# First keys of a hybrid layer's memory projection: one transfer or two, and their place in two queues

## The chip, the cores and the metric

The kernel runs on one core of a Trainium2 chip. The metric is the device time of one execution in microseconds. TensorE (PE in the profile, its weight loads PEld) multiplies; VectorE is DVE, ScalarE ACT, GpSimd POOL; SyncE (SP) issues most of the DMA transfers. A line such as L445 is a line of the kernel before.

## The reference, cut to what matters

```python
h = rms_norm(x, norm_g)                      # x: 256 tokens of 1024 channels
(qa, ka, va, ga, ub, vb, gb, qc, gc, ma, mb, mc) = split_cols(h @ w_in, IN_SPLITS)
out_a = moba_attention(rope(qa), rope(ka), va) * silu(ga)          # 6 heads
out_b = gmlp_spatial_gate(ub, vb, ln_g, w_spatial, b_spatial) * silu(gb)
mk, mv = split(rms_norm(mem, mem_norm_g) @ w_mem_kv, 2, axis=-1)   # 256 memory tokens, 2 x 512 columns
out_c = softmax(qc @ mk.T * 128 ** -0.5) @ mv * silu(gc)           # 4 heads
y = sigmoid(ma) * (out_a @ w_a) + sigmoid(mb) * (out_b @ w_b) + sigmoid(mc) * (out_c @ w_c)
out = rms_norm(x + y @ w_out, final_norm_g)
```

All is float32. The change concerns the loads for the product of the memory tokens with `w_mem_kv`, whose left half of columns gives the memory's keys (mk) and whose right half its values (mv), and one piece of `w_in`.

## The kernel before, in words

Every float32 product is made from three passes: each operand is split into a high part that TensorE takes at its fast float32 format (ACT copies it, "hi") and the remainder (DVE subtracts, "lo"), and high x high, high x low and low x high are summed in PSUM. So each slice of weights goes through the same string: it lands by DMA, ACT makes its high part, DVE its low part, TensorE uses both.

The work is a list of 128 chunks, worked off in order by TensorE. Chunks 0 to 7 ("mvk") are the memory's keys and values: the 1024 channels are cut into 8 slices of 128, and HALVES gives the order of value and key slices: chunk 0 is the first values and the first keys, chunk 1 the second values and keys, and so on. Chunks 8 to 11 ("tok") and all later ones multiply the layer's own tokens with pieces of `w_in` ("fea" chunks, 128 output columns each, and "st" chunks, which form products of two-by-two blocks from seven factors), then come the three branch products and the output product.

A slice of the array `mw` holds, for 128 channels, 256 memory tokens, 512 value columns and 512 key columns (slice 0 has 16 columns of gains ahead of them). Tokens and values go to the tile `st` (two tiles, of four slices each, by `load_st`, L311), the keys to the first raw pieces, `raw[2]` and `raw[3]` (by `load_wk`, L325 and, for the last two slices together, L323). Slice 0's tokens and values come in two transfers, the tokens with the first 256 value columns on SP's queue and the other 256 on ACT's. Slice 1's tokens and values (384 KB) come on ACT's queue, everything else on SP's, in the order in which the loop at the end of this section's listing issues it: keys of slice 0, keys of slice 1, then for each further slice the tokens and values and then the keys, with two rows of x in between.

In the first chunks `split_mvk` makes the engines' work: the memory tokens are multiplied with their gains and split (DVE in chunks 0 to 2: L435 the high part, L430 the low part; later ACT makes the high part at L427), and `half_hi` (ACT, L445) and `half_lo` (DVE, L449) split the values and the keys. For chunk 0 `half_hi` works on two halves of 256 columns. TensorE multiplies values at L525 (into the banks "aux") and keys at L531 (into "acc"). While the first load is under way TensorE runs eight matmuls on constants (L377).

The other pieces of `w_in` ("raw", 128 rows of 2048 columns, two chunks each, 1 MB) are loaded by `load` at L220 into three buffers as these come free; pieces 12 to 21 come as two halves of 512 KB, the others whole. Piece 12 holds the "fea" chunks q4 and k4, and `split_hi` at L274 makes their high parts. The order of all this work behind the first chunks is set when the program is built by a planner (`Units`) with its own estimates of durations; it knows nothing of the transfers of the first slices but a few fixed times.

Each DMA issued by SP or ACT is given one of eight landing semaphores (DMAHW0 to DMAHW7) in turn. An issue that gets a semaphore for a second time waits until the transfer that had it before has landed.

Of the kernel before, what the change touches and what calls it, by code (L numbers as in the profile page):

```python
# [42 lines left out]
NG = 2 * KD  # L43
# [110 lines left out]
def tile_hybrid_layer(ctx: ExitStack, tc: tile.TileContext, mw, xT, mem, x, fin_g, ln_g, w, ws, w_sp, b_sp, b_spt, rope, out):  # L154
    nc = tc.nc
# [9 lines left out]
    def slot_tile(name, shape, tag, dt=F32):  # L165
        V[name] = act.tile(shape, dt, name=name, tag=tag)
        return V[name]
# [22 lines left out]
    raw, hi, lo = {}, {}, {}  # L190
# [24 lines left out]
    def raw_alloc(j):  # L215
        raw[j] = wts.tile([128, PIECE], F32, name="raw", tag="raw", bufs=RAW)

    def load_part(j, a, b):
        src = bass.AP(tensor=w.tensor, offset=w.offset + (j - 4) * 128 * PITCH + a, ap=[[PITCH, 128], [1, b - a]])
        nc.sync.dma_start(raw[j][:, a:b], src)  # L220

    def load(j):
        raw_alloc(j)
        parts = 2 if 12 <= j < 22 else 1
        for i in range(parts):
            load_part(j, i * PIECE // parts, (i + 1) * PIECE // parts)

# [25 lines left out]
    def buf(g, i):  # L253
        return FORMS[i][0] ^ (g % 2)
# [36 lines left out]
    XW = S + 512  # L291
# [8 lines left out]
    def slice_k(k, a, b):  # L300

        row = NG + XW + 512
        return bass.AP(tensor=mw.tensor, offset=mw.offset + 128 * row * k + a, ap=[[row, 128], [1, b - a]])

    def load_st(queue, k, a, b):

        o = 0 if k < 4 else -NG - 4 * XW
        a, b = (a and a + NG, b + NG) if k == 0 else (a, b)
        src = slice_k(k, a, b)
        o += NG + k * XW if k else 0  # L310
        queue.dma_start(st[k // 4][:, o + a:o + b], src)  # L311
# [5 lines left out]
    def load_wk(queue, k):  # L317
        o = XW if k else NG + XW
        if k == KD - 1:
            row = NG + XW + 512  # L320
            src = bass.AP(tensor=mw.tensor, offset=mw.offset + 128 * row * (k - 1) + o,
                          ap=[[row, 128], [128 * row, 2], [1, 512]])
            queue.dma_start(raw[3][:, 1024:2048].rearrange("p (k n) -> p k n", k=2), src)  # L323
        elif k < KD - 2:
            queue.dma_start(raw[2 + k // 4][:, (k % 4) * 512:(k % 4) * 512 + 512], slice_k(k, o, o + 512))  # L325

    def load_x(parts=1):
        slot_tile("xk", [128, 2, D], "xr")
        for i in range(parts):
            rows = slice(2 * i // parts, 2 * (i + 1) // parts)  # L330
            nc.sync.dma_start(V["xk"][:, rows, :], x[:, 0:2 * D].rearrange("p (t d) -> p t d", t=2)[:, rows, :])

    def load_x_row(t):
        if t == 0:
            slot_tile("xk", [128, 2, D], "mr")
        nc.sync.dma_start(V["xk"][:, t, :], x[:, t * D:t * D + D])
# [8 lines left out]
    load_st(nc.sync, 0, 0, S + 256)  # L345
    load_st(nc.scalar, 0, S + 256, XW)
    nc.scalar.preload_act_table(AF.Sqrt)
    load_st(nc.scalar, 1, 0, XW)
    for k in range(KD):
        if k > 1:  # L350
            load_st(nc.sync, k, 0, XW)
        load_wk(nc.sync, k)
        if k in (4, 5):
            load_x_row(k - 4)
    load_xt(0)
# [890 lines left out]
    for c in range(n_br):  # L1246
        if chunks[c][0] == "st":
            _, g, i, h = chunks[c]
            b = buf(g, i)
# [5 lines left out]
    for c in range(n_br + 4):  # L1255
# [4 lines left out]
        if c == n_br - 8:  # L1260
            load_x()
# [21 lines left out]
        for d in (0, LATER) if s in place else ():  # L1283
            q, odd = divmod(2 * place[s][0] + place[s][1] - 1 - d, 2)
            q += 2
            if not odd and 4 < q < len(PLAIN) // 2 and (q in LATE) == (d > 0):
                load(q)
                if q == 6:
                    load_mem()
# [132 lines left out]
```

## Time and profile before

| | |
|---|---|
| median of 3 runs | 312.42 us (312.19 to 313.19) |
| the profiled execution's own time | 311.98 us |
| its span | 310.3 us |
| PE busy | 304.0 us, 98% |
| PEld busy | 258.5 us, 83% |
| DVE busy | 269.5 us, 87% |
| ACT busy | 232.6 us, 75% |
| mean granted TensorE clock | 0.996 |

The span runs from the first to the last instruction; the execution's own time has some microseconds around it. In a timeline's row stand the start, the busy time, the engine, the line, the operation and out<-in; brackets give the engine's idle time ahead of it and what ended that. An engine's name with a q (SPq, ACTq) is its sequencer, which issues DMAs. The chain of work that ended last is followed back from the last instruction, at each step to what released it.

### The profile page before, as it was taken

What the parts mean: (1) busy time and instruction counts of PE and PEld (TensorE: products, weight loads), DVE (VectorE), ACT (ScalarE), POOL (GpSimd) and SP (SyncE); (2) the same over time, 40 slices, a digit from 0 to 9 for tenths busy, and PEclk for the clock granted to TensorE, in tenths of its full rate; (3) what the DMA queues carried; (4) which work ended last, traced back from release to release, by engine and by line L of the source; (5) the groups of instructions that cost most, each with busy time, mean ns of one, the idle gap of its engine ahead of it and who ended that gap; (6) DMA issues with size and microseconds to landing.
All of it is one profiled execution on the core that took longest, in us unless ns stands there. A gap on an engine that the chain in (4) does not pass through costs nothing.

```text
span 310.3 us, 4528 instructions
## 1 busy us (share of the span) xinstructions
PE 304.0 (98%) x1570; PEld 258.5 (83%) x1570; DVE 269.5 (87%) x391; ACT 232.6 (75%) x373; POOL 35.8 (12%) x55
## 2 busy tenths in 40 slices
PE   8999999999999999999999999999999999999993
PEld 4888888889888888888888888888888888888982
DVE  3989999899879999898699899999896898989532
ACT  5877999766797865888999996698659666586333
POOL 1000040040011013005013002004011031000022
PEclk9999999999999999999999999999999999999998
DMA  7999999659959869959949959969996999953003
GB/s 283 396 407 413 419 281 299 247 82 183 371 191 274 251 212 208 286 201 208 343 125 196 259 230 278 212 219 209 210 374 126 296 328 219 372 207 136 2 0 135
DMA packets 20598, 75.14 MB, mean 242 GB/s; under 512 B 2656, under 2 KB 3936, under 8 KB 18144
## 3 DMA queue, kind: packets, MB, share of 16 engines
q1 hardware_dynamic: 15824, 58.35, 51.5%
q0 software_dynamic: 4320, 15.73, 28.2%
q10 hardware_dynamic: 432, 0.79, 0.7%
q8 instruction: 12, 0.20, 0.2%
q14 instruction: 10, 0.08, 0.1%
HBM read 73.02 MB, written 1.05 MB: 239 GB/s over the span
## 4 chain that ended last, share of the span: by engine, by line
PE 97%; DMA 1%; ACT 1%; issue 0%; DVE 0%; ACTq 0%
PE acc L658 27%; PE acc L593 19%; PE aux L593 12%; PE acc L471 6%; PE acc L473 6%; PE acc L472 6%; PE acc L531 4%; PE aux L525 4%; PE aux L472 2%; PE aux L473 2%; PE aux L471 2%; PE aux L825 2%; PE acc L504 2%; PE aux L504 2%; DMA st<-in_mw_dram 1%; PE aux L1058 1%
## 5 line engine op out<-in xcount | busy, mean ns | idle before, releaser
L274 ACT ACTIVATE hi<-form 128x1024 fp32r<-128x1024 f32 x70 | 73.0, 1059 | 32.4 <-DMA form<-in_ws_dram 17.9
L277 DVE TENSOR_TENSOR lo<-form,hi 128x1024 fp32r<-128x1024 f32 x70 | 84.4, 1219 | 11.7 <-ACT hi L274 11.6
L277 DVE TENSOR_TENSOR lo<-raw,hi 128x1024 fp32r<-128x1024 f32 x58 | 70.1, 1221 | 6.5 <-ACT hi L274 6.2
L274 ACT ACTIVATE hi<-raw 128x1024 fp32r<-128x1024 f32 x58 | 61.1, 1059 | 9.9 <-PE acc L473 4.8
L658 PE MATMUL acc<-n,hi 128*128 128x512 f32 x240 | 59.8, 392 | 0.0
L244 POOL DMA_DIRECT2D form<-in_ws_dram x30 | 26.1, 875 | 225.1 <-DVE lo L277 78.6
L658 PEld LDWEIGHTS acc<-n,hi 128*128 128x128 f32 x240 | 44.1, 188 | 8.6
L658 PEld LDWEIGHTS acc<-n,lo 128*128 128x128 f32 x240 | 31.4, 191 | 1.4
L658 PE MATMUL acc<-n,lo 128*128 128x256 f32 x240 | 32.5, 283 | 0.0
L593 PE MATMUL acc<-hi,s 128*128 128x512 f32 x96 | 32.3, 394 | 0.0
L593 PE MATMUL acc<-hi,n 128*128 128x512 f32 x72 | 24.2, 395 | 0.0
L593 PEld LDWEIGHTS acc<-hi,s 128*128 128x128 f32 x96 | 18.0, 188 | 3.5
L593 PE MATMUL aux<-hi,s 128*128 128x512 f32 x64 | 20.7, 389 | 0.0
L593 PE MATMUL acc<-lo,s 128*128 128x512 f32 x48 | 18.7, 390 | 0.0
L593 PE MATMUL aux<-hi,n 128*128 128x512 f32 x48 | 15.9, 391 | 0.0
L593 PEld LDWEIGHTS acc<-hi,n 128*128 128x128 f32 x72 | 13.5, 188 | 2.7
L593 PEld LDWEIGHTS aux<-hi,s 128*128 128x128 f32 x64 | 12.0, 188 | 2.6
L593 PE MATMUL acc<-lo,n 128*128 128x512 f32 x36 | 14.1, 390 | 0.0
L593 PE MATMUL aux<-lo,s 128*128 128x512 f32 x32 | 12.5, 389 | 0.0
L248 DVE TENSOR_TENSOR form<-form,form 128x1024 f32<-128x1024 f32 x10 | 12.2, 1219 | 0.0
L593 PEld LDWEIGHTS aux<-hi,n 128*128 128x128 f32 x48 | 9.0, 188 | 1.8
L593 PEld LDWEIGHTS acc<-lo,s 128*128 128x128 f32 x48 | 9.0, 188 | 1.5
(262 smaller groups left out, 607.5 us busy)
## 6 DMA issues: line engine op xcount, KB each, us to landing
raw<-in_w_dram SPq DMA_DIRECT2D x18, 1024.0 KB, 8.2
form<-in_ws_dram SPq DMA_DIRECT2D x30, 512.0 KB, 5.4
form<-in_ws_dram POOLq DMA_DIRECT2D x30, 512.0 KB, 8.6
raw<-in_w_dram SPq DMA_DIRECT2D x22, 512.0 KB, 6.9
st<-in_mw_dram SPq DMA_DIRECT2D x6, 384.0 KB, 6.7
raw<-in_mw_dram SPq DMA_DIRECT2D x6, 256.0 KB, 5.6
xk<-in_x_dram SPq DMA_DIRECT2D x2, 512.0 KB, 6.9
xt<-in_xT_dram SPq DMA_DIRECT2D x2, 512.0 KB, 8.9
```

Of the source, the lines that this page charges most:

```text
L244: nc.gpsimd.dma_start(form_half(i, h), block(g, b, h), accum_op=OP.add)
L248: nc.vector.tensor_tensor(form_half(i, h), form_half(i, h), form_half(1 - i, h), OP.add)
L274: nc.scalar.activation(hi[c][:, a:b], source(c)[:, a:b], AF.Copy)
L277: nc.vector.tensor_tensor(lo[c][:, a:b], source(c)[:, a:b], hi[c][:, a:b].bitcast(F32), OP.subtract)
L471: nc.tensor.matmul(p, s_hi, m_hi, start=first, stop=False)
L472: nc.tensor.matmul(p, s_hi, m_lo, start=False, stop=False)
L473: nc.tensor.matmul(p, s_lo, m_hi, start=False, stop=last)
L504: nc.tensor.matmul(acc[name, o][t], src[:, k0 + i, tsl(t)], wt[c][:, i * 512:(i + 1) * 512], start=c == 8 and i + j == 0, stop=c == 11 and ...
L525: nc.tensor.matmul(acc["mv", 0][t][:, a:b], src[:, k, tsl(t)], wt[:, a:b], start=k + n == 0, stop=k == KD - 1 and n == len(parts) - 1)
L531: nc.tensor.matmul(p, wt, m, start=k == 0 and j < HC, stop=k == KD - 1 and j >= HC)
L593: nc.tensor.matmul(p, x[:, k0 + k, tsl(t)], wt[c][:, a * 512:(a + 1) * 512], start=first and a + j == 0, stop=half == 1 and a + j == 3, sk ...
L658: nc.tensor.matmul(o, wt, m, start=i == 0, stop=i == len(passes) - 1, skip_group_check=True)
```

## The change

The first slice's keys, one transfer of 256 KB on SP's queue before, become two of 128 KB: columns 0 to 255 on SP's queue, columns 256 to 511 on ACT's. On ACT's queue that half stands ahead of the second slice's tokens and values. And piece 12 of `w_in` is loaded whole, as one transfer of 1 MB, where it came in two.

```diff
     def load(j):
         raw_alloc(j)
-        parts = 2 if 12 <= j < 22 else 1
+        parts = 2 if 13 <= j < 22 else 1
...
+    def load_wk_first(queue, a, b):
+        queue.dma_start(raw[2][:, a:b], slice_k(0, NG + XW + a, NG + XW + b))
+
...
     load_st(nc.sync, 0, 0, S + 256)
     load_st(nc.scalar, 0, S + 256, XW)
     nc.scalar.preload_act_table(AF.Sqrt)
+    load_wk_first(nc.sync, 0, 256)
+    load_wk_first(nc.scalar, 256, 512)
     load_st(nc.scalar, 1, 0, XW)
     for k in range(KD):
         if k > 1:
             load_st(nc.sync, k, 0, XW)
-        load_wk(nc.sync, k)
+        if k:
+            load_wk(nc.sync, k)
```

How the instructions stand: on SP, the program's first loads before, with the semaphores that each issue waits for in brackets (`st` are tokens and values, `raw` the keys, 528 columns are slice 0's gains, tokens and first values):

```order
L311 DMA st_72<-in_mw_dram 128x528
L325 DMA raw<-in_mw_dram 128x512 x2
L311 DMA st_72<-in_mw_dram 128x768
L325 DMA raw<-in_mw_dram 128x512
L311 DMA st_72<-in_mw_dram 128x768
L325 DMA raw<-in_mw_dram 128x512 [waits DMAHW0_49]
L311 DMA st_73<-in_mw_dram 128x768 [waits DMAHW1_49]
```

And the same place on SP now:

```order
L311 DMA st_72<-in_mw_dram 128x528
L328 DMA raw<-in_mw_dram 128x256
L325 DMA raw<-in_mw_dram 128x512
L311 DMA st_72<-in_mw_dram 128x768
L325 DMA raw<-in_mw_dram 128x512
L311 DMA st_72<-in_mw_dram 128x768 [waits DMAHW0_49]
L325 DMA raw<-in_mw_dram 128x512 [waits DMAHW1_49]
```

The first key transfer has half its columns. With one transfer more in the turn of the eight semaphores, the first issue that waits is the fourth slice's tokens and values (it waits for slice 0's second transfer), where it was the fourth slice's keys. On ACT, the program's start before (its queue and its work; the two DMAs are slice 0's other values and slice 1):

```order
L311 DMA st_72<-in_mw_dram 128x256
L347 ACT_TABLE_LOAD
L311 DMA st_72<-in_mw_dram 128x768
L445 ACTIVATE hi<-st_72 128x256 [waits DMAHW1_49]
L445 ACTIVATE hi<-st_72 128x256 [waits DMAHW0_49]
L445 ACTIVATE hi<-raw 128x256 [waits DMAHW2_49]
L445 ACTIVATE hi<-raw 128x256
L445 ACTIVATE hi<-st_72 128x512 [waits DMAHW4_49]
```

And the same place on ACT now:

```order
L311 DMA st_72<-in_mw_dram 128x256
L350 ACT_TABLE_LOAD
L328 DMA raw<-in_mw_dram 128x256
L311 DMA st_72<-in_mw_dram 128x768
L451 ACTIVATE hi<-st_72 128x256 [waits DMAHW1_49]
L451 ACTIVATE hi<-st_72 128x256 [waits DMAHW0_49]
L451 ACTIVATE hi<-raw 128x256 [waits DMAHW2_49]
L451 ACTIVATE hi<-raw 128x256 [waits DMAHW4_49]
L451 ACTIVATE hi<-st_72 128x512 [waits DMAHW6_49]
```

ACT issues one DMA more, ahead of slice 1; its work stands in the same order, and the second half of the first keys now waits for a landing of its own. On SP around piece 12 (`form` are sums of weight blocks, `mid` the rotary embedding's moves):

```order
 L220 DMA raw<-in_w_dram 128x2048 x2
-L241 DMA form_403<-in_ws_dram 128x1024
+L241 DMA form_404<-in_ws_dram 128x1024
+L220 DMA raw<-in_w_dram 128x2048
+L241 DMA form_404<-in_ws_dram 128x1024
+L819 DMA mid<-qk 32x256 x4
 L220 DMA raw<-in_w_dram 128x1024 x2
-L241 DMA form_403<-in_ws_dram 128x1024
-L813 DMA mid<-qk 32x256 x4
```

Piece 12 is one issue of 2048 columns at the same place; what follows stands as before (the next pair of halves is piece 13).

## The prediction

> **What bounds the kernel now.** I read the page's busy times first, then the list of waits of TensorE's weight loads, then the chain of work that ended last over the first 12 us, and only then the single engines in that stretch.
>
> ```profile
> span 310.3 us, 4528 instructions
> PE 304.0 (98%) x1570; PEld 258.5 (83%) x1570; DVE 269.5 (87%) x391; ACT 232.6 (75%) x373; POOL 35.8 (12%) x55
> ```
>
> TensorE is busy for 98% of the span, so a change to loads can only win where TensorE waits for them. The waits of its weight loads from 0 to 300 us say where that is (columns: total us, times, longest):
>
> ```profile
> PEld L377 <- issue: 2.5, 7, 0.8
> PEld aux L525 <- ACT hi L445: 0.7, 1, 0.7
> PEld acc L531 <- DVE lo L449: 0.3, 1, 0.3
> PEld acc L531 <- ACT hi L445: 0.3, 1, 0.3
> PEld aux L525 <- DVE lo L449: 0.2, 1, 0.2
> ```
>
> L377 is the warming up. The other four are all there are, and the chain (start, length, what) puts them at the start:
>
> ```profile
> 0.81 2.95 DMA st<-in_mw_dram
> 3.78 0.43 ACT hi L445
> 4.28 1.76 PE aux L525 x8
> 6.04 1.62 PE acc L531 x8
> 7.66 1.40 PE aux L525 x6
> 9.06 1.39 PE acc L531 x8
> 10.45 1.37 PE aux L525 x6
> ```
>
> L525 is a slice of the values, L531 a slice of the keys. Undisturbed they take 1.37 and 1.39 (the last two rows). So the first values lose 1.76 - 1.37 = 0.39 us, the first keys 1.62 - 1.39 = 0.23, the second values 0.03: 0.65 us in all, and that is everything that faster first loads could give after the first landing. The next rows are the weight loads, then ACT and DVE of the same stretch:
>
> ```profile
> 5.88 0.75 PEld L531 LDWEIGHTS acc<-m,hi 128*128 128x128 f32 x4 [0.28 <-ACT hi L445]
> 6.91 0.54 PEld L531 LDWEIGHTS acc<-m,lo 128*128 128x128 f32 x4 [0.28 <-DVE lo L449]
> 7.38 0.78 PEld L525 LDWEIGHTS aux<-hi,m 128*128 128x128 f32 x4
> 8.30 0.33 PEld L525 LDWEIGHTS aux<-lo,m 128*128 128x128 f32 x2
> ...
> 3.78 0.72 ACT L445 ACTIVATE hi<-st 128x256 fp32r<-128x256 f32 x2 [1.25 <-DMA st<-in_mw_dram]
> 5.41 0.73 ACT L445 ACTIVATE hi<-raw 128x256 fp32r<-128x256 f32 x2 [0.91 <-DMA raw<-in_mw_dram]
> 6.04 0.62 ACT L445 ACTIVATE hi<-st 128x512 fp32r<-128x512 f32 x1
> ...
> 4.57 0.69 DVE L449 TENSOR_TENSOR lo<-st,hi 128x512 fp32r<-128x512 f32 x1
> 6.17 0.69 DVE L449 TENSOR_TENSOR lo<-raw,hi 128x512 fp32r<-128x512 f32 x1 [0.91 <-ACT hi L445]
> 6.78 0.35 DVE L435 TENSOR_SCALAR m<-st 128x256 fp32r<-128x256 f32 x1
> 7.16 0.48 DVE L430 SCALAR_TENSOR_TENSOR m<-st,m 128x256 fp32r<-128x256 f32 x1
> 7.56 0.68 DVE L449 TENSOR_TENSOR lo<-st,hi 128x512 fp32r<-128x512 f32 x1
> ```
>
> The reader is to see the string: the first keys land, ACT (idle for 0.91) splits off their high part from 5.41 to 6.14, DVE (idle for 0.91) the low part from 6.17 to 6.86, and TensorE waits 0.28 us for each. A weight load of 0.19 follows the last one every 0.23, so 0.04 of each 0.28 is ordinary: the keys' lateness costs 2 x 0.24 = 0.48 us. The second slice's low part is just in time too (7.56 + 0.68 = 8.24, loaded at 8.30).
>
> **The change part by part.** First, when things land. The landings' rows (KB, then us from issue to landing) and the issues:
>
> ```profile
> 0.80 0.41 ACTq L311 DMA_DIRECT2D st<-in_mw_dram  x1
> 0.81 0.38 SPq L311 DMA_DIRECT2D st<-in_mw_dram  x1
> 1.25 0.89 SPq L325 DMA_DIRECT2D raw<-in_mw_dram  x2
> 1.25 1.28 ACT L347 ACT_TABLE_LOAD   x1 [1.25 <-PEq L1411]
> 1.28 0.42 ACTq L311 DMA_DIRECT2D st<-in_mw_dram  x1
> 2.18 0.43 SPq L311 DMA_DIRECT2D st<-in_mw_dram  x1
> ...
> 3.15 0.43 SPq L311 DMA_DIRECT2D st<-in_mw_dram  x1
> ...
> st<-in_mw_dram ACTq DMA_DIRECT2D x1, 384.0 KB, 4.3
> ...
> st<-in_mw_dram ACTq DMA_DIRECT2D x1, 128.0 KB, 3.2
> ...
> raw<-in_mw_dram SPq DMA_DIRECT2D x1, 256.0 KB, 4.1
> ...
> raw<-in_mw_dram SPq DMA_DIRECT2D x1, 256.0 KB, 4.5
> ...
> st<-in_mw_dram SPq DMA_DIRECT2D x1, 384.0 KB, 5.2
> ```
>
> The 256 KB with 4.1 are the first keys (issued 1.25, landed 5.4), those with 4.5 the second keys (the second of the two issues, at about 1.7: 6.2). The second slice's tokens and values, 384 KB on ACT's queue, land at 1.28 + 4.3 = 5.6; the third slice's at 2.18 + 5.2 = 7.4. Behind their queues' heads the first keys end SP's first 264 + 256 = 520 KB and the second slice ACT's first 128 + 384 = 512 KB, and they land within 0.2 us of each other: the two queues advance about evenly. So landing goes by the bytes ahead on both: 1032 KB by 5.5, 1288 KB (the second keys: 776 on SP, 512 on ACT) by 6.2, 1672 KB by 7.4, some 340 KB per us.
>
> After the change the first keys' halves end SP's first 392 KB and ACT's first 256: at most 784 KB with the other queue's share, 248 less than the 1032 of before. 248 / 340 = 0.7 us earlier, about 4.7 instead of 5.4 (an estimate from these landings). The second slice now ends ACT's first 640 KB: 1280 KB in all if the queues stay even, which landed at 6.2; if SP's queue runs ahead by its earlier start, some 1350 to 1400 KB, 6.5. I take 6.4, between the two; the outer bounds are 6.2 and the third slice's 7.4. The second keys and all later loads have the same bytes ahead as before and stay.
>
> The keys: ACT has done the first values at 3.78 + 0.72 = 4.50, so it splits the keys from 4.7 to 5.4, DVE, free at 5.26, to 6.1. TensorE without its 0.24 asks for the high part at 5.64 and without 0.48 for the low part at 6.43: both are there. Gain 0.48.
>
> The second slice: TensorE now asks for it at 7.38 - 0.48 = 6.90. Landed at 6.4, its high part is done at 6.4 + 0.03 + 0.62, and 0.04 of handing over gives 7.1: 0.2 of the gain is lost again, 0.28 stays. Its low part takes DVE from 6.43 as long as from 6.78 to 8.24, 1.46, so 7.9, for a load due 0.92 after 7.1, at 8.0: in time. That load came at 8.30 before, so 0.3 us stays from here on. With a landing at 6.2 it is 0.5, at 6.5 it is 0.2, at 6.7 nothing, and later it is a loss.
>
> Other costs at the head are nothing: the additional issue of 0.42 us on ACT lies between 1.7 and 2.1, and ACT's first work starts at 3.78 (the issue at 1.28 went out beside the table load of 1.28 us, so the table doesn't hold the queue; if it did, the second slice would be issued at 2.5 instead of 1.7, still before its turn). SP's fourth slice now waits for slice 0's second transfer (issued 0.80, landed 3.2 later), so it is issued at 4.0 instead of 3.15; SP's queue then has data up to the third keys (1672 + 256 = 1928 KB, 8.1 at 340 KB per us) in front of it, so it doesn't run dry; were that cover gone, the fourth slice would come up to 0.9 late.
>
> The whole piece 12 (the fea weights q4 and k4): the two halves now, and the first reading of them:
>
> ```profile
> 74.17 1.41 SPq L220 DMA_DIRECT2D raw<-in_w_dram  x2
> ...
> raw<-in_w_dram SPq DMA_DIRECT2D x1, 512.0 KB, 7.8
> ...
> 92.46 1.11 ACT L274 ACTIVATE hi<-raw 128x1024 fp32r<-128x1024 f32 x1
> ```
>
> The first half landed at 74.17 + 7.8 = 82.0 and was read at 92.46. Whole, it comes with the second half, some 1.5 us later (512 KB at 340 KB per us): 9 us of cover remain, and SP saves one issue while it stands in front of a wait for DVE anyway. Zero; without its cover it would cost those 1.5 us.
>
> Does 0.3 us at 8 us reach the end? After 8.30 TensorE has no wait in the list, and the engines that feed it wait for it in their turn, for instance:
>
> ```profile
> 57.75 0.38 ACT L671 ACTIVATE qk<-acc 128x256 f32<-128x256 f32 x1 [1.45 <-PE acc L658]
> ```
>
> so they come along. The sum: 0.48 - 0.2 + 0.02 = 0.3 us off the profiled execution's own 311.98 (its span 310.3 and 1.7 around it), 311.7. The median of the runs shown is 312.42, 0.44 above that execution: 312.1 for the median. About 0.3%, 0.94 us, is what a measurement of this kernel can tell from no change (the three runs shown lie within 1.00), so this is no change.
>
> One rule speaks against the change. The Trainium skill, "DMA: Bandwidth & Descriptors", section "Issuing engines are not separate DMA queues", says that transfers issued from several engines run on the same 16 DMA engines and interleave, so that a second queue saves only the issuing time. By it the sum would be 0 instead of 0.3. The even advance of the two queues above agrees that they share one stream; whether order within the stream then helps is what no row of before shows.
>
> **The rivals.** (1) The halves come no sooner: they interleave with everything else and the later one lands at 5.4 as now. Then ACT's string is the old one, the second slice at 6.4 is still before the 6.7 at which it hurts, and the gain is 0: 312.4. For it: both queues are in one stream. Against it: 248 KB now stand behind the keys that stood beside them.
>
> (2) Slower: the second slice becomes the wait. The place is TensorE's load at 7.38 (L525), the engine ahead of it ACT's 0.62 us. It decides from a landing of 6.7 on, and each us later costs one. If ACT's queue gets less than its turn once SP's longer rows stand against it, the slice lands with the third one at 7.4: 0.7 lost, 313.1. Only past 7.6 would it be told from no change. Against it: the even advance so far.
>
> (3) The whole gain: the second slice lands at 6.2 or before, and TensorE keeps all but the first values' 0.18: 0.5, 311.9.
>
> (4) Something later gives more than 0.9 us either way, as a shifted order of transfers; the list of waits, empty after 8.3, speaks against it.
>
> **How the numbers follow.** My forecast (a gain of 0.1 to 0.4) has 0.5, rival 3 has 0.17, rival 1 0.17, rival 2 0.1 (a fourth of it beyond 0.9), rival 4 0.06. All but rival 4 and that part of rival 2 are within 0.3%: same 0.9; faster 0.05 (most of rival 4 and of the runs' own spread), slower 0.05. The range: from the lowest run shown with all 0.65 us won, 312.19 - 0.65 = 311.5, to rival 2's 313.1.
>
> **What would show it.** Right: ACT's first reading of the keys at 4.6 to 4.9 instead of 5.41; the two waits of 0.3 under L531 gone from the list, and in their place one of 0.1 to 0.3 us of the second values for ACT; the chain's second values starting about 7.1 to 7.4 (7.66 before) and the slice after that 0.3 earlier; ACT's reading of piece 12 without a wait for its landing. Wrong: the keys still at 5.4, a wait of DVE or ACT for the second slice past 6.7, or a wait of TensorE anywhere after 9 us.

## The result, and the profile after

| | before | after |
|---|---|---|
| median of 6 runs each, same chip | 312.26 us (312.18 to 313.19) | 313.98 us (313.47 to 315.06) |
| ratio, 95% interval | | 1.0051 [1.0037, 1.0065] |
| the profiled execution's own time | 311.98 us | 315.06 us |
| its span | 310.3 us | 313.4 us |

The changed kernel is slower by 1.7 us in the median, where no change (312.1) was forecast; the time lies outside the forecast range (311.5 to 313.1). The profiled execution is the longest of the six, so its events show more of the effect than a usual run does.

The busy times of the page after the change:

```profile
span 313.4 us, 4527 instructions
PE 305.0 (97%) x1570; PEld 259.2 (83%) x1570; DVE 269.1 (86%) x391; ACT 231.7 (74%) x373; POOL 35.7 (11%) x55
```

The work is the same within a us on each engine; the 3.1 us are waiting. The waits of TensorE's weight loads from 0 to 300 us (total us, times, longest; L531 are the values, L537 the keys, L525 and L531 before):

```profile
PEld aux L531 <- ACT hi L451: 3.1, 2, 2.3
PEld L383 <- issue: 2.5, 7, 0.8
PEld aux L599 <- DVE obl L1093: 0.6, 1, 0.6
```

Both waits of the keys (two of 0.3 before) are gone, as forecast. The values' wait for ACT's high part has grown from one of 0.7 to two of 3.1 together, the longest 2.3. The chain that ended last, over the first 13 us:

```profile
1.72 7.62 DMA st<-in_mw_dram
9.34 0.02 issue
9.36 0.64 ACT hi L451
10.00 0.04 issue
10.04 1.66 PE aux L531 x6
11.71 1.39 PE acc L537 x8
```

The chain no longer begins with the first tokens (0.81 before) but with the second slice's tokens and values: issued at 1.72, landed at 9.34, 5.59 before. ACT's timeline around it shows both halves of the matter:

```profile
3.93 0.72 ACT L451 ACTIVATE hi<-st 128x256 fp32r<-128x256 f32 x2 [1.40 <-DMA st<-in_mw_dram]
4.56 0.71 ACT L451 ACTIVATE hi<-raw 128x256 fp32r<-128x256 f32 x2
9.36 0.63 ACT L451 ACTIVATE hi<-st 128x512 fp32r<-128x512 f32 x1 [4.10 <-DMA st<-in_mw_dram]
```

ACT reads the first keys at 4.56 without waiting (5.41 before, after 0.91 of idle time), and then sits idle for 4.10 us. TensorE's weight loads:

```profile
6.22 0.88 PEld L537 LDWEIGHTS acc<-m,hi 128*128 128x128 f32 x4
7.14 0.65 PEld L537 LDWEIGHTS acc<-m,lo 128*128 128x128 f32 x4
10.04 0.76 PEld L531 LDWEIGHTS aux<-hi,m 128*128 128x128 f32 x4 [2.25 <-ACT hi L451]
```

The keys are loaded in one piece, and the second values come at 10.04, 2.66 us after the 7.38 of before. The landings (KB, us from issue):

```profile
st<-in_mw_dram ACTq DMA_DIRECT2D x1, 384.0 KB, 7.6
...
raw<-in_mw_dram SPq DMA_DIRECT2D x1, 128.0 KB, 3.3
raw<-in_mw_dram ACTq DMA_DIRECT2D x1, 128.0 KB, 3.4
```

The two halves land after 3.3 and 3.4 us, at 4.51 and 4.68 (forecast 4.7). The second slice takes 7.6 us, 4.3 before. Last, the stretch from 4 to 6 us in one row (busy times, clock, DMA share, GB/s), of the kernel before:

```profile
4.00:6.00 2.00, 1.89 (x10) 1.25 (x10) 1.22 (x3) 1.09 (x4) 0.00 (x0) 1.00 1.03 388
```

and of the changed one:

```profile
4.00:6.00 2.00, 1.98 (x8) 1.52 (x8) 1.97 (x4) 1.26 (x4) 0.00 (x0) 1.00 0.93 322
```

The transfers move 322 GB/s there instead of 388, some 130 KB less in these two us; at the prediction's 340 KB per us that is 0.4 us, too little for a landing 3 us late. The rest shows in the landing's single steps. In the traces each transfer raises its semaphore 16 times, and the waiting work starts after the last raise (9.34, ACT at 9.36). I read each raise as one of the 16 DMA engines that has done its part; the trace doesn't name them. These are the raises of the second slice's transfer in us, in order:

```
before 5.14 5.20 5.21 5.23 5.24 5.25 5.26 5.27 5.28 5.32 5.37 5.41 5.48 5.49 5.56 5.59
after  5.92 6.01 6.08 6.09 6.10 6.15 6.21 6.30 6.31 6.37 6.53 7.08 7.21 7.24 8.55 9.34
```

Half of the DMA engines are done by 6.30, about the time that the bytes gave (6.4). Five come 0.8 to 3.0 us after the eighth, and the landing is the last of them. The other queue has the same: the second keys, on SP's, landed at 8.09 (6.24 before), with five raises from 6.88 on, and the third slice at 9.53 (7.40 before).

### The profile page after: what moved, and what is told of

Its sections match the earlier page's. It is cut to its first block, busy times and chain, and to the rows that moved or that the text cites. A ratio compares the mean times of both kernels' runs of the same rounds, so it can differ in the third digit from the quotient of the medians.

```text
span 313.4 us, 4527 instructions
## 1 busy us (share of the span) xinstructions
PE 305.0 (97%) x1570; PEld 259.2 (83%) x1570; DVE 269.1 (86%) x391; ACT 231.7 (74%) x373; POOL 35.7 (11%) x55
## 4 chain that ended last, share of the span: by engine, by line
PE 80%; DMA 7%; ACT 5%; issue 4%; DVE 2%; POOL 0%; ACTq 0%; POOLq 0%
PE acc L664 20%; PE acc L599 14%; PE aux L599 11%; PE acc L478 6%; PE acc L479 6%; PE acc L477 6%; DMA form<-in_ws_dram 5%; PE aux L531 3%; PE acc L537 3%; DMA st<-in_mw_dram 2%; PE aux L478 2%; PE aux L479 2%; PE aux L477 2%; ACT hi L274 2%; PE acc L510 2%
## 5 line engine op out<-in xcount | busy, mean ns | idle before, releaser
L599 PE MATMUL acc<-hi,s 128*128 128x512 f32 x96 | 32.3, 394 | 0.0
L599 PE MATMUL acc<-hi,n 128*128 128x512 f32 x72 | 24.2, 395 | 0.0
L599 PE MATMUL aux<-hi,s 128*128 128x512 f32 x64 | 20.8, 391 | 0.1
L599 PEld LDWEIGHTS acc<-hi,s 128*128 128x128 f32 x96 | 18.0, 188 | 3.5
L599 PE MATMUL acc<-lo,s 128*128 128x512 f32 x48 | 18.7, 390 | 0.0
L599 PE MATMUL aux<-hi,n 128*128 128x512 f32 x48 | 15.8, 391 | 0.0
L599 PEld LDWEIGHTS acc<-hi,n 128*128 128x128 f32 x72 | 13.5, 188 | 2.7
L599 PEld LDWEIGHTS aux<-hi,s 128*128 128x128 f32 x64 | 12.0, 188 | 3.0 <-DVE obl L1093 0.6
L599 PE MATMUL acc<-lo,n 128*128 128x512 f32 x36 | 14.1, 390 | 0.0
L599 PE MATMUL aux<-lo,s 128*128 128x512 f32 x32 | 12.5, 389 | 0.0
L531 PE MATMUL aux<-hi,m 128*128 128x512 f32 (+1 forms) x34 | 9.3, 404 | 2.1 <-ACT hi L451 2.1
L599 PEld LDWEIGHTS aux<-hi,n 128*128 128x128 f32 x48 | 9.0, 188 | 1.8
```

What stands on the lines that cost most here:

```text
L531: nc.tensor.matmul(acc["mv", 0][t][:, a:b], src[:, k, tsl(t)], wt[:, a:b], start=k + n == 0, stop=k == KD - 1 and n == len(parts) - 1)
L599: nc.tensor.matmul(p, x[:, k0 + k, tsl(t)], wt[c][:, a * 512:(a + 1) * 512], start=first and a + j == 0, stop=half == 1 and a + j == 3, sk ...
```

## The experiments

Sixteen kernels, each timed in five rounds against the kernel before on the same chip. Diffs under "the changed head" are against the changed kernel, and piece 12 comes in halves there; the others are against the kernel before. Single letters in the expectations are the names of theories, each described where it is used; P is one theory in "both halves on SP" and "third slice ahead" and another in the last two. A theory that held for long, H, reads: rows of what is issued at about 1.7 us or later reach the DMA engines only some 2.5 us after, and if the first two transfers on SP's and ACT's queue hold too few bytes to last till then, DMA engines run short.

The table gives, for the profiled execution: KB in the first two transfers of SP's and ACT's queues together, GB/s from 4 to 6 us, when the eighth and when the last DMA engine finished the second slice's transfer (its last part, where it is cut), the span, and then the ratio of the timed runs. One profiled execution is not always a usual one: with the slice on SP's queue it is longer than the median (313.66 us for 312.94), with the key pairs it is the longest of 12 (315.80 for 313.58), with the first transfer cut the shortest of 12 (312.97 for 314.20).

| kernel | KB | GB/s | 8th | last | span | ratio, 95% |
|---|---|---|---|---|---|---|
| before | 1032 | 388 | 5.27 | 5.59 | 310.3 | |
| piece 12 whole only | 1032 | 373 | 5.38 | 5.88 | 310.7 | 0.9988 [0.9974, 1.0002] |
| slice issued later | 1032 | 368 | 5.36 | 5.94 | 310.5 | 1.0009 [0.9995, 1.0023] |
| both halves on SP | 904 | 356 | 5.00 | 5.30 | 310.6 | 1.001 [0.9992, 1.0027] |
| first transfer cut | 776 | 349 | 4.70 | 4.99 | 311.2 | 1.005 [1.0032, 1.0069] |
| slice cut, large part first | 904 | 377 | 6.13 | 7.00 | 311.2 | 1.0029 [1.0015, 1.0042] |
| whole keys on ACT | 904 | 395 | 7.17 | 7.59 | 311.2 | 1.003 [1.0018, 1.0043] |
| key pairs | 904 | 386 | 7.44 | 8.85 | 314.1 | 1.003 [1.0017, 1.0042] |
| slice cut, tokens first | 776 | 340 | 6.12 | 7.77 | 311.8 | 1.0062 [1.0041, 1.0084] |
| the change | 648 | 322 | 6.30 | 9.34 | 313.4 | 1.0051 [1.0037, 1.0065] |
| head only | 648 | 320 | 6.31 | 9.16 | 313.4 | 1.0055 [1.0032, 1.0077] |
| third slice ahead | 648 | 314 | 6.57 | 8.81 | 313.3 | 1.0054 [1.0032, 1.0077] |
| halves by rows | 648 | 291 | 7.32 | 8.01 | 312.3 | 1.0064 [1.0044, 1.0083] |
| slice on SP | 648 | 287 | 5.41 | 7.34 | 311.9 | 1.0007 [0.9994, 1.002] |
| both halves on ACT | 776 | 286 | 8.05 | 9.59 | 313.7 | 1.0089 [1.0069, 1.0109] |
| slice by GpSimd | 648 | 277 | 7.04 | 8.15 | 312.1 | 1.0033 [1.0018, 1.0049] |
| slice by GpSimd, whole keys | 648 | 296 | 6.37 | 8.26 | 312.0 | 1.0029 [1.0016, 1.0041] |
| slice by GpSimd, first | 648 | 321 | 5.56 | 7.53 | 311.1 | 1.0026 [1.0015, 1.0038] |

### Which part of the change

Head only, the changed head with nothing else:

```diff
-        parts = 2 if 13 <= j < 22 else 1
+        parts = 2 if 12 <= j < 22 else 1
```

> The first keys in two halves as in the changed kernel, piece 12 in two halves as before. The changed kernel's trace has the second slice's tokens and values landing at 9.3 us (5.6 before) and TensorE waiting 2.3 us for them. If that head is the whole of the loss, this run keeps it: ratio 1.004 to 1.007, a wait of more than 1 us at the second values. If the whole piece 12 makes the loss or a part of it, the ratio is below 1.002.

Piece only, on the kernel before:

```diff
-        parts = 2 if 12 <= j < 22 else 1
+        parts = 2 if 13 <= j < 22 else 1
```

> Only piece 12 is loaded whole; the first loads are those of before. If the head is the cause: ratio 0.999 to 1.001, no wait of TensorE past 9 us. If the whole piece is the cause: 1.003 to 1.007 and a wait near 92 to 105 us.

The head alone gives the whole loss (1.0055), the piece alone nothing that can be told (0.9988). What is left is the head.

### Which of its two steps: the halves, or the place ahead of the second slice

The changed head with both halves on SP's queue, so that the second slice stays ACT's second transfer:

```diff
-    load_wk_first(nc.scalar, 256, 512)
+    load_wk_first(nc.sync, 256, 512)
```

> Both halves of the first keys go on SP's queue, so that the second slice stays ACT's second transfer. Theory D (both queues are drained of short rows at the same time, about 4.0 us, and some DMA engines then stand without work until the next transfers' rows are there): ACT's queue holds long rows then, no DMA engine stands idle, the second slice lands at 5.5 to 5.8, ratio 0.999 to 1.001. Theory S (rows of 1 KB themselves are the trouble): ratio above 1.003. Theory P (the second slice's tokens and values and the second keys, neighbours in the same rows of memory, are read side by side and disturb each other): they are less side by side here, so ratio below 1.002.

The landing rows of that kernel:

```profile
st<-in_mw_dram ACTq DMA_DIRECT2D x1, 384.0 KB, 4.0
...
raw<-in_mw_dram SPq DMA_DIRECT2D x2, 128.0 KB, 3.7
```

The second slice lands at 5.30, the halves at 4.76 and 5.63, and the time is that of before (1.001). Cutting the keys in two costs nothing here that can be told; the suspicion falls on the place that the second slice loses. The changed head with the whole keys, not cut, on ACT's queue ahead of it:

```diff
-    load_wk_first(nc.sync, 0, 256)
-    load_wk_first(nc.scalar, 256, 512)
+    load_wk_first(nc.scalar, 0, 512)
```

> The first keys as one transfer of 256 KB on ACT's queue, ahead of the second slice's tokens and values; SP's second transfer is the second keys (256 KB). Theory D: the two queues hold 0.23 MB more ahead of their third transfers, which are issued at the same 1.7 us and are needed 0.5 us later, so few or no DMA engines run dry: no landing spread over 1 us, the second slice at 7.2 to 7.6 by its bytes, TensorE waits 0.5 to 0.8 for it: ratio 1.000 to 1.003. If what hurts is any third transfer on ACT's queue, the slice lands past 8.5 and the ratio is above 1.004.

Its landing rows:

```profile
st<-in_mw_dram ACTq DMA_DIRECT2D x1, 384.0 KB, 5.9
...
raw<-in_mw_dram ACTq DMA_DIRECT2D x1, 256.0 KB, 3.9
```

The keys land at 5.20, the slice at 7.59, with all its DMA engines within 0.6 us (6.99 to 7.59) and 395 GB/s. Here is lateness by order alone: the slice behind 384 KB of its own queue, and SP's third transfer beside it (7.39) ahead of it. It costs 0.3%, and the rate shows no shortage.

### What keeps single DMA engines back

The changed head with the third slice's tokens and values ahead of the second keys on SP's queue, in case rows of neighbouring places were in each other's way:

```diff
-        if k:
+        if k == 2:
+            load_wk(nc.sync, 1)
+        if k > 1:
             load_wk(nc.sync, k)
```

> As the changed kernel's head (piece 12 in halves), but on SP the third slice's tokens and values go ahead of the second keys, so that the second slice's tokens and values on ACT's queue run beside another slice's rows. Theory P: the stragglers go, the second slice lands at 6.2 to 6.6, ratio 0.998 to 1.001. Theory D: nothing changes at 4.0 us, ratio 1.004 to 1.007 with a landing past 7.5.

The changed head with halves by rows (the function then takes partitions a to b with all 512 columns, 2 KB each), in case it was the short rows of 1 KB:

```diff
-    load_wk_first(nc.sync, 0, 256)
-    load_wk_first(nc.scalar, 256, 512)
+    load_wk_first(nc.sync, 0, 64)
+    load_wk_first(nc.scalar, 64, 128)
```

> As the changed kernel's head (piece 12 in halves), but the first keys are cut by partitions: 64 rows of 2 KB on each queue instead of 128 rows of 1 KB. Theory D (both queues are drained at about 4.0 us, before the rows of the next transfers, issued at 1.7 us, are there on all DMA engines): the same bytes are drained at the same time, so the second slice still lands past 7.5 and the ratio is 1.003 to 1.007. Theory S (the short rows of 1 KB are the trouble): landing at 6.2 to 6.6, ratio 0.998 to 1.001.

The changed head with the second slice as SP's third transfer, and then with both halves on ACT's queue, in case it mattered that both queues came to the same place together:

```diff
-    load_st(nc.scalar, 1, 0, XW)
+    load_st(nc.sync, 1, 0, XW)
```

> As the changed kernel's head (piece 12 in halves), but the second slice's tokens and values are SP's third transfer, and ACT's queue ends with its half of the keys. Theory D as it stands (the next rows are not there at 4.0 us, whichever queue): DMA engines still stand idle from 4.0 us, landing past 7, ratio above 1.002. Theory Q (it is two queues that go over to new transfers at the same time): one queue alone goes over, the slice lands at 5.6 to 6.0, the keys at 4.6, TensorE loses neither: 0.5 us won, ratio 0.997 to 0.9995.

```diff
-    load_wk_first(nc.sync, 0, 256)
+    load_wk_first(nc.scalar, 0, 256)
```

> Both halves of the first keys on ACT's queue ahead of the second slice, SP's second transfer is the second keys with rows of 2 KB. Theory D: SP's rows cover the moment at which ACT's queue goes over to its next transfer, no DMA engine stands idle at 4.0 us; the second slice lands at 6.5 to 7.2, TensorE waits 0.1 to 0.5 for it and wins 0.5 at the keys: ratio 0.999 to 1.001. Theory S (short rows): stragglers as in the changed kernel, ratio above 1.003.

None of these removes it: 286 to 314 GB/s, and a last DMA engine 0.7 to 2.2 us behind the eighth. So the loss of rate needs neither the neighbouring rows, nor rows of 1 KB, nor two queues in step. (With halves by rows the picture is another one: the eighth DMA engine too is late, 7.32.) Both halves on ACT were expected about as fast as before by theory D and were the slowest of all; only S had a loss there. The second half of the keys, ACT's third transfer, landed at 8.00, the slice, its fourth, at 9.59, and TensorE waits for both; for the keys:

```profile
PEld acc L537 <- ACT hi L451: 1.4, 1, 1.4
```

The slice on SP is back at the time of before (1.0007): 15 of 16 DMA engines were done by 6.31, the last at 7.34. That is neither D's loss nor Q's gain.

The slice by GpSimd, behind that engine's first small fills, once with the changed head and once on the kernel before with its whole keys:

```diff
-    load_st(nc.scalar, 1, 0, XW)
...
+    load_st(nc.gpsimd, 1, 0, XW)
```

> As the changed kernel's head (piece 12 in halves), but the second slice's tokens and values are issued by GpSimd, as its first transfer, at about 1.8 us; ACT's queue ends with its half of the keys. Theory H (the third transfer of a queue has its rows on the DMA engines only from about 4.4 us on; what the first two of each queue hold, 648 KB here as in the changed kernel, is drained at 4.0): a third source has rows by then, no DMA engine stands idle at 4 to 5 us, the slice lands at 5.5 to 6.5, the keys at 4.5 to 4.9: ratio 0.997 to 1.000. If the halves of the keys hurt by themselves: stragglers and a ratio above 1.003.

> The kernel before with its keys whole on SP's queue, and the second slice's tokens and values issued by GpSimd at about 1.8 us. Theory H: the first keys have only ACT's 128 KB beside them and land at 4.6 to 5.0 (5.4 before) without being cut; GpSimd's rows cover the time to SP's third transfer, the second slice lands at 5.6 to 6.5: ratio 0.997 to 1.000. If GpSimd's rows come late (past 5), the slice lands past 6.7 and the ratio is above 1.001.

Neither gave what a queue of its own was hoped to give. The landing row with the changed head (issued at 1.71):

```profile
st<-in_mw_dram POOLq DMA_DIRECT2D x1, 384.0 KB, 6.4
```

The slice landed at 8.15, and at 8.26 with the whole keys, where H had 5.5 to 6.5 for both. The second of the two shows something else: its keys, whole and on SP as before, landed at 4.58, 5.39 before. So they came early without being cut, once the second slice didn't stand beside them.

The kernel before with only the second slice cut, tokens (128 KB) as ACT's second transfer, values (256 KB) as its third:

```diff
-    load_st(nc.scalar, 1, 0, XW)
+    load_st(nc.scalar, 1, 0, S)
+    load_st(nc.scalar, 1, S, XW)
```

> The kernel before, with its keys whole and where they were, but the second slice's tokens (128 KB) and values (256 KB) are two transfers on ACT's queue. Theory H: the first two transfers of each queue hold 264 + 256 + 128 + 128 = 776 KB, as little as in the run with both halves on ACT, so DMA engines stand idle between 4.1 and 5.5, the values of the second slice land past 7 and the ratio is 1.002 to 1.009, though nothing of the keys is changed. If it is the keys' halves, or the keys ahead of the second slice, that hurt: no idle DMA engines, landing at 5.6 to 6.4, ratio 0.999 to 1.001.

The chain of that kernel has the same wait as the changed kernel's:

```profile
1.72 6.05 DMA st<-in_mw_dram
7.77 0.02 issue
7.79 0.64 ACT hi L446
```

And its stretch from 4 to 6 us is slow:

```profile
4.00:6.00 2.00, 2.00 (x8) 1.63 (x8) 1.49 (x4) 1.20 (x4) 0.00 (x0) 1.00 1.01 340
```

With the keys untouched, cutting the second slice alone costs as much as the change (1.0062). H had foreseen it, so the next kernels were made against H. First the changed head with the slice as GpSimd's first issue (at 1.34, where 0.8 was expected, instead of 1.71), which brings what is issued by 1.7 us to 1032 KB:

```diff
     load_st(nc.scalar, 0, S + 256, XW)
+    load_st(nc.gpsimd, 1, 0, XW)
...
-    load_st(nc.scalar, 1, 0, XW)
```

> The changed head (halves of the first keys on both queues, piece 12 in halves), with the second slice's tokens and values as GpSimd's first issue, at about 0.8 instead of 1.7 us. Theory H, that rows of whatever is issued at 1.7 us are on the DMA engines only from about 4.2 us and what was issued before must last until then: now 264 + 128 + 128 + 128 + 384 = 1032 KB are issued by 1.7, as many as before the change, so 4 to 6 us move at least 700 KB (before 776, changed kernel 643), the second slice has landed by 6.7, TensorE's wait for its high part is at most 0.3 us, and the ratio is 0.998 to 1.002 (first tokens up to 0.3 us later count against it). Rival G, that GpSimd's transfers are slow to start by themselves and the 2.7 us from issue to first row seen with the issue at 1.71 is the queue's own: rows from about 3.5, still in time for the engines, but the second slice lands at 6.7 to 7.5, ratio 1.001 to 1.004. Rival R, that it is the two halves themselves that leave the engines short, whatever is issued beside them: under 680 KB from 4 to 6 us, landing past 7.5, ratio 1.003 to 1.007.

GpSimd's timeline has the issue:

```profile
1.34 0.74 POOL L311 DMA_DIRECT2D st<-in_mw_dram  x1 [0.83 <-POOLq L1417]
```

And the stretch from 4 to 6 us:

```profile
4.00:6.00 2.00, 1.77 (x10) 1.36 (x10) 1.91 (x4) 1.22 (x4) 0.00 (x0) 1.00 0.93 321
```

H fails here (321 GB/s, landing 7.53), unless GpSimd's bytes aren't counted. The time (1.0026) is that of the rival that GpSimd's transfers are slow to begin: the first row is moved at 3.9, 2.6 us after the issue, on a queue with nothing ahead of it.

Second, the changed head with halves on both queues, but in pairs with the second slice's keys, so that the second transfers hold 256 KB each:

```diff
-        queue.dma_start(raw[2][:, a:b], slice_k(0, NG + XW + a, NG + XW + b))
+        src = bass.AP(tensor=mw.tensor, offset=mw.offset + NG + XW + a,
+                      ap=[[row, 128], [128 * row - NG, 2], [1, b - a]])
+        queue.dma_start(raw[2][:, 0:1024].rearrange("p (k n) -> p k n", k=2)[:, :, a:b], src)
...
-        if k:
+        if k > 1:
             load_wk(nc.sync, k)
```

> As the changed kernel (piece 12 in halves), but each queue's second transfer brings its half of the columns of the first and the second slice's keys, 256 KB instead of 128; the second keys have no transfer of their own. The halves stand on both queues and the second slice's tokens and values are ACT's third transfer, as in the changed kernel, but the first two transfers of both queues hold 264 + 256 + 128 + 256 = 904 KB. Theory H, that the DMA engines run short when these hold 776 KB or less and not from 904 on: 350 GB/s or more from 4 to 6 us (before 388, changed 322), the second slice lands at 6.0 to 6.8 and on no DMA engine far behind the others, ratio 0.998 to 1.002. Rival R, that halves on both queues, or a second slice in ACT's third place, run short by themselves: under 345 GB/s, landing past 7.5, ratio 1.003 to 1.007.

Its chain:

```profile
1.75 7.10 DMA st<-in_mw_dram
8.85 0.02 issue
8.87 0.64 ACT hi L454
```

Its stretch from 4 to 6 us:

```profile
4.00:6.00 2.00, 1.79 (x10) 1.38 (x10) 1.28 (x4) 1.28 (x4) 0.00 (x0) 1.00 1.04 386
```

Each side is right in one half: the DMA engines don't run short (386), as H has it, and the slice is late all the same. Fifteen DMA engines bring it at 7.19 to 7.75, as with the whole keys on ACT, by order; the last comes at 8.85. So in this execution a single DMA engine is 1.1 us late though the rate shows no shortage. Third, the kernel before with only slice 0's first transfer cut:

```diff
-    load_st(nc.sync, 0, 0, S + 256)
+    load_st(nc.sync, 0, 0, S)
+    load_st(nc.sync, 0, S, S + 256)
```

> The kernel before, keys whole on SP and the second slice ACT's second transfer, both untouched; only slice 0's first transfer on SP's queue is cut in two, tokens (136 KB) and the first 256 value columns (128 KB), so that the keys become SP's third transfer. The first two transfers of both queues then hold 264 + 512 = 776 KB. Theory H: the DMA engines run short (at most 345 GB/s from 4 to 6 us), the keys are late on some DMA engines and land at 6 to 8 (5.4 before), TensorE waits for them, ratio 1.002 to 1.007. Rival B, that one queue with enough rows (ACT's 512 KB) keeps the engines busy, or that it takes a late second slice: 355 GB/s or more, keys at 5.4 to 5.7, ratio 0.999 to 1.001.

Its chain:

```profile
1.24 3.25 DMA st<-in_mw_dram
4.50 0.02 issue
4.52 0.42 ACT hi L446
```

Its stretch from 4 to 6 us:

```profile
4.00:6.00 2.00, 1.33 (x7) 0.83 (x6) 1.12 (x2) 0.99 (x3) 0.00 (x0) 1.00 1.01 349
```

The keys land at 5.71, on no DMA engine far behind the others: H's 6 to 8 is a miss, and 349 GB/s lies between the two sides' bounds. The kernel is slower (1.005) with a wait that neither side had named: the first values now are a second transfer and land at 4.50 instead of 3.76, and TensorE waits 1.5 us for them, 0.7 before. That is the 0.9 us of this execution's span; the further 1.2 us of the median stand in no trace.

The last two ask whether it is the bytes, the place on the queue or the time of issue. The second slice cut with the large part first:

```diff
-    load_st(nc.scalar, 1, 0, XW)
+    load_st(nc.scalar, 1, 0, 2 * S)
+    load_st(nc.scalar, 1, 2 * S, XW)
```

> The kernel before with the second slice's transfer cut in two on ACT's queue, as in the kernel with tokens and values apart, but the large part first: 256 KB (tokens and half of the values) as ACT's second transfer and the last 128 KB as its third, issued at about 1.72. Theory H, by bytes: the first two transfers of both queues hold 264 + 256 + 128 + 256 = 904 KB, the DMA engines don't run short (355 GB/s or more from 4 to 6 us, before 388), the last part lands at 5.6 to 6.2, ratio 0.999 to 1.001. Rival P, by place or time: what ACT issues third, at 1.72, is late whatever it is: it lands past 7, ratio 1.002 to 1.006.

And the second slice whole in its old place, but held back by a fill of zeros under it:

```diff
+    nc.gpsimd.memset(st_k(1, 0, XW), 0.0)
     load_st(nc.scalar, 1, 0, XW)
```

> The kernel before with the same transfers in the same places; but GpSimd first fills the second slice's room with zeros (which the transfer then overwrites), so that ACT issues it some 0.45 us later, at about 1.7 instead of 1.28, still as its second transfer. Theory T, by time: rows issued at about 1.7 are on the DMA engines only from 4.2 us; what was issued by 1.3 holds 264 + 128 + 256 = 648 KB, so the engines run short (at most 345 GB/s from 4 to 6 us), the second slice lands past 7, ratio 1.002 to 1.006. Rival P, by place: second on its queue it is not late beyond its 0.45 us: landing 5.6 to 6.2, 355 GB/s or more, ratio 0.999 to 1.001.

The issue in ACT's timeline of this last kernel:

```profile
1.57 0.33 ACTq L311 DMA_DIRECT2D st<-in_mw_dram  x1
```

And its stretch from 4 to 6 us:

```profile
4.00:6.00 2.00, 1.55 (x9) 1.13 (x8) 1.44 (x3) 1.02 (x3) 0.00 (x0) 1.00 1.04 368
```

Cut, its last 128 KB land at 7.00, 14 of 16 DMA engines by 6.47; the ratio 1.0029 is that of the rival by place, though the bytes were there and the rate shows no shortage (377). Held back to 1.57 (less than the planned 1.7, so that the theory by time isn't fully tried), it lands at 5.94 and costs nothing that can be told.

### What follows

In the 18 kernels the second slice has landed by 5.94 where it is whole and ACT's second transfer, and at 7.0 or later in every other place. Two things are seen in that. One is order: behind 384 KB of its own queue, with SP's third transfer beside it, it comes at 7.0 to 7.6 with 377 and 395 GB/s. The other is the spread: in eight of the eleven kernels with 648 or 776 KB the last DMA engine is 1.5 to 3 us behind the eighth. Of the seven with 904 or 1032 KB one has 1.4 and the others 0.3 to 0.9. From 4 to 6 us all kernels with 904 KB or more moved at least 356 GB/s, all with 776 or less at most 349; but 349 and 356 lie close, and the key pairs show lateness at 386.

The packets in the traces, each a row of a transfer, show two things more. On average 13.9 of them were under way at once from 4 to 5 us in the changed kernel, 16.5 in the kernel before, so about two of the 16 DMA engines stood empty. And single rows took long: of the rows begun from 3 to 9 us the longest took 1.29 us in the changed kernel and 0.40 in the kernel before, 0.76 to 1.64 in the eleven kernels with 776 KB or less, 0.35 to 0.73 in the seven others. So both happen, and both go with few bytes at the head of the queues. That they come from few bytes is not shown, nor what makes a row take so long; and as packets carry no DMA engine's name, whether the late ones are those with the long rows stays open.

No version was told from the kernel before as faster; the piece alone comes nearest.

## Why the prediction was wrong

**What bounds the kernel, and where a us counts**: right. The decision at 6.7 and one us for each us later held about: landed 2.6 us past 6.7, the second values are loaded 2.66 us late, and the span is 3.1 us longer, and the wait at L599 for DVE (0.6) is about the size of what is left. In the table, spans are 310.3 to 310.7 with landings of 5.30 to 5.94 and rise to 313.7 at 9.59; the key pairs (314.1 at 8.85) lie above that, and the first transfer cut (311.2 at 4.99) has its loss elsewhere.

**The keys**: right. 4.51 and 4.68 where 4.7 stood, ACT at 4.56, DVE's low part done at 6.01 (6.1), the two waits gone. By the rule of the Trainium skill that was weighed there ("DMA: Bandwidth & Descriptors", section "Issuing engines are not separate DMA queues") the gain would have been 0; the trace agrees with 16 DMA engines for both queues so far as each transfer has 16 raises, but not with the sum that was drawn from it: order inside the stream moved the keys by 0.7 to 0.9 us. The rival of no sooner keys is out.

**The second slice**: here the prediction failed. "I take 6.4, between the two; the outer bounds are 6.2 and the third slice's 7.4" is a landing worked out from bytes at a steady 340 KB per us. That gave the middle of the 16 DMA engines (6.30); the step that failed is the one from there to the landing, which took for granted that all 16 always have rows and are done at about the same time, as in the kernel before. The last came at 9.34. The median is 1.1 us shorter than the profiled execution, so at one us for each us a usual run has it at about 8.3 (an estimate), still past 7.4. The lower rate, 322 GB/s, is 0.4 us of that; the rest are five late engines. "The second keys and all later loads have the same bytes ahead as before and stay" failed in the same way (8.09 for 6.24, 9.53 for 7.40). The prediction asked only of SP's queue whether it "doesn't run dry", and at 8 us, not of the DMA engines at 4.

That the queues "advance about evenly" was read from one pair of landings and is not what failed here, but it is no rule either: with the slice cut, large part first, ACT's first 512 KB were done on eight DMA engines at 6.13, 5.27 before. Why single DMA engines are late stays open.

**Rival 2**: the right wait, place and threshold, with a price that was too low (landing 7.4 and 313.1, against 9.34 in the profile and 313.98 in the median) and a chance of 0.1. Its reason, that ACT's queue gets less than its turn, is not what the raises show: the middle one was in time, and SP's second keys were spread too. Its price stopped at the third slice's landing of before, 7.4, as if that were fixed; in the changed kernel the third slice itself came at 9.53.

**Piece 12**: zero, as forecast. **The carry to the end**: right, and as true for a loss as for a gain. Rivals 3 and 4 played no part.

## What to carry to other kernels

Moving a small load ahead moves another one back: before the gain is counted, find the load that loses its place and its slack (here 1.1 us, from 5.6 to 6.7), and try the change without that displacement, as with both halves on SP. A landing forecast from bytes and a mean rate was here that of the middle DMA engine; the wait ends with the last of 16, which in these first 10 us of the program came 0.3 to 3 us later, so such a load needs that much slack.

## What the runs showed of the hardware

- One transfer's 16 parts finished within 0.5 us in the kernel before (5.14 to 5.59) and over 3.4 us in the changed one (5.92 to 9.34), with the same bytes.
- Cutting a transfer wasn't free: cutting 384 KB into 128 and 256 on the same queue, with no other load changed, made the last part land 2.2 us later (7.77 for 5.59); cut as 256 and 128, 1.4 later (7.00).
- A transfer that GpSimd issued at 1.34 on an empty queue moved its first row at 3.9; in the same kernel those that SP and ACT issued at 0.80 moved theirs at 1.82 and 2.16.
